# Two-layer hybrid encoder: late accumulating transfers behind a GpSimd copy, another order of two block products, halved memory attention, and small moves at the start and the end

## The chip, the cores and the metric

The kernel runs on one core of a Trainium2 chip. The metric is the device time of one execution in microseconds; the median of several runs counts. "PE" is the matrix engine, "PEld" its weight loads, DVE, ACT and POOL are the vector, scalar and GpSimd engines, and SP is the engine that only issues transfers. All shapes are partitions x elements, in float32 unless said otherwise.

## The reference

The reference computes two layers on 512 positions of width 2048. Each layer does, for h = rmsnorm(x):

```python
z = h @ w_in[l]                                   # 2048 -> 4928 columns
q_lat, kv_lat, k_pe, gb, gc, xin, q_mem, gate = split_cols(z)
a_out = mla_attention(q, k, v)                    # 8 heads over 512 keys, from the latents
c_out = short_gated_conv(gb, gc, xin, conv_w[l])  # gb * conv3(gc * xin)
m_out = memory_attention(q_mem, mem_n, w_mk, w_mv)  # 4 heads over 256 memory tokens
y = concatenate([a_out, c_out, m_out]) * silu(gate)
x = x + rmsnorm(y @ w_o[l])
```

The change leaves what is computed as it is.

## The kernel before, in words

**Numbers in two parts.** Each float32 operand of a matmul is split: ACT rounds it ("hi", `wh` for weights, line 212), DVE subtracts to get the rest ("lo", `wl`, line 216), and PE sums three products (`mm3s`, line 298).

**Units.** A unit is 256 rows of a weight block of 512 (or 416) columns, held as one 128x1024 tile `wr` of the pool `raw` (8 buffers). It costs PE 12 matmuls of 512 columns. `Program.run` goes through the steps in order; before a step it issues loads some units ahead (`load`, on the SP queue) and rounds units two steps ahead (`prep`). `wh` and `wl` have three buffers each, so rounding is also held to PE's pace.

**Seven products.** Every projection pair (five per layer) and both output projections multiply 2x2 blocks with seven products, P1 to P7, of four units each, instead of eight (`group`, line 473). The right-hand operands are sums of weight blocks. P5, P6 and P4 share the four tiles T: a second block is added to T in place before each use. For P7 the sum is a DVE addition of a freshly loaded tile (line 200); for P6 and P4 it is a transfer with accumulation that GpSimd issues (`more`, line 165). It is issued as soon as the earlier user of T is rounded (lines 217 to 218). The left-hand operands (S1 to S4, sums of activations) are made by deferred steps (`combine`), which `pr.until` forces out when a product needs them. P3 and P7 of one pair are interleaved unit by unit: P3 of rows 0, P7 of rows 0, P3 of rows 1, and so on; they share the tile B22, which P7 adds to after P3 has used it. The lists FIRST, HEAD and STEADY (lines 467 to 469) give the order of the products of a projection pair; SECOND and FOUR are those of the output projection.

**Order of engines.** PE, SP and POOL follow the written order. DVE and ACT are ordered by the scheduler of the framework, except at the start and in the output projection. Each engine's instructions run in order.

**Start.** `setup` builds an identity and issues five small constant transfers on ACT's queue. `first_load` (line 663) fetches x in half rows on SP; x tile 1 follows the squares of tile 0 in the program.

**Attention.** `head_iters` (line 1064) runs score, transposition and product with the values as a pipeline: scores of iteration k, transpositions of iteration k-3, and the product with V of the head that finished at k-5. The last rope head does that product in two halves of 256 queries (`halves`, line 1067).

**End.** `residual` (line 1301) normalises a 128-row tile of the output and adds it to x in two parts of 1024 columns. For the last tile the second part goes in two parts of 512, from a copy `o2` (lines 1268 to 1270).

Of the kernel before, what the change touches and what calls it, by code (L numbers as in the profile page):

```python
# [5 lines left out]
F32 = mybir.dt.float32  # L6
# [3 lines left out]
ALU = mybir.AluOpType  # L10
AX = mybir.AxisListType

P = 128
# [3 lines left out]
NT = S // P  # L17
MT = 256
HEADS = 8
# [44 lines left out]
class Unit:  # L64
# [2 lines left out]

    def __init__(self, key, loads=(), more=None, plus=None, alloc=None, gain=None, keep=None, other=None):  # L70
        self.key = key
        self.loads = loads
        self.more = more
        self.plus = plus
        self.alloc = alloc
        self.gain = gain
        self.keep = keep
        self.other = other
        self.behind = None


class Program:
# [40 lines left out]
    def run(self):  # L123
# [7 lines left out]
            users.setdefault(u.key, []).append(c)  # L131
        after = {a: b for cs in users.values() for a, b in zip(cs, cs[1:])}
        first_more = [c for c, u in enumerate(seq) if u.more is not None and users[u.key][0] == c]

        def move(engine, t, off, src, **kw):
            n = 1
# [51 lines left out]
        def prep(upto):  # L188
            while at["prep"] < min(upto, len(seq)):
                c = at["prep"]  # L190
                load(c + 1)
                while first_more and first_more[0] <= c + self.more_ahead:
                    load(first_more[0] + 1)
                    more(first_more.pop(0))
                u = seq[c]
                src = tiles[u.key]
                if any(e[0] == u.key for e in late):
                    flush()
                if u.plus is not None:
                    nc.vector.tensor_tensor(src, src, tiles[c], op=ALU.add)  # L200
                if u.other is not None:
                    nc.vector.tensor_tensor(src, src, tiles[u.other], op=ALU.add)
                at["prep"] += 1
                n = src.shape[-1]
                if u.alloc is None:
                    hi = hip.tile([P, 1024], F32R, tag="wh", name=f"wh{c}")
                    lo = lop.tile([P, 1024], F32R, tag="wl", name=f"wl{c}")
                else:
                    hi, lo = u.alloc()
                outs[c] = (hi[:, :n], lo[:, :n])  # L210
                if u.gain is None:
                    nc.scalar.copy(hi[:, :n], src)  # L212
                    flush()

                    def rest(c=c, n=n, src=src, hi=hi, lo=lo):
                        nc.vector.tensor_tensor(lo[:, :n], src, hi[:, :n].bitcast(F32), op=ALU.subtract)  # L216
                        if c in after and seq[after[c]].more is not None:
                            more(after[c])
                    late.append((u.key, rest))
                    if not self.lag:  # L220
                        flush()
                else:
                    flush()
                    for k, g in enumerate(u.gain()):
                        h = slice(k * (n // 2), (k + 1) * (n // 2))
                        nc.scalar.activation(hi[:, h], src[:, h], AF.Copy, scale=g)  # L226
                        nc.vector.scalar_tensor_tensor(lo[:, h], src[:, h], g, hi[:, h].bitcast(F32),  # L227
                                                       op0=ALU.mult, op1=ALU.subtract)
# [23 lines left out]
def encoder(tc, x, mem, positions, pre_norm_g, w_in, q_norm_g, w_uq, kv_norm_g, w_ukv, conv_w,  # L252
# [17 lines left out]
    banks = pool("banks", bufs=8, space=bass.MemoryType.PSUM)  # L270
    dram = pool("dram", space=bass.MemoryType.DRAM)
    pr = Program(nc, raw_p, hi_p, lo_p)
    add = pr.add

    G = {}
# [197 lines left out]
    def group(left, key, w, block, slot, passes, final, hold=None, by_two=False):  # L473
# [9 lines left out]
        def unit(q, c):  # L483
            def of(name, *loads, more=None, plus=None, alloc=None, **kw):
                return Unit((key, name, c), [block(h, j, c) for h, j in loads],
                            None if more is None else block(*more, c), None if plus is None else block(*plus, c), alloc,
                            **kw)
            if passes is FOUR and q in ("P5", "P6", "P7"):
                return {"P5": lambda: of("T", more=(0, 1)), "P6": lambda: of("T", other=(key, "B22", c)),
                        "P7": lambda: of("B22", plus=(0, 1))}[q]()  # L490
            if q == "P1":
                return of("P1" if apart else "T", (0, 0))
            if q == "P5":
                if passes is FIRST:
                    return of("T", (0, 0), more=(0, 1))
                return of("T", *([(0, 0)] if apart else []), plus=(0, 1))
            return {"P6": lambda: of("T", more=(1, 1)), "P4": lambda: of("T", more=(1, 0), alloc=hold),
                    "P2": lambda: of("P2", (1, 0)), "P3": lambda: of("B22", (1, 1)),
                    "P7": lambda: of("B22", plus=(0, 1))}[q]()

# [58 lines left out]
        def step(q, c):  # L559
            def f(*ops):  # L560
                if c == 0:
                    banks_for(q)
                if c < 3:
                    mm3s([p for tt in range(2) for p in products(q, c, tt, ops[0])])
                    return
                for tt in range(2):
                    mm3s(products(q, c, tt, ops[0]))
                    pr.flush()
                    ended(q, tt)
            return f  # L570
# [34 lines left out]
        for k, names in enumerate(passes):  # L605
            if names == ["P4"] and hold:
                for c in range(2):
                    out[2].insert(9 + 3 * c, (lambda ops, c=c: kept.__setitem__(c, ops), [unit("P4", c)], 0.0))
                out.append([(piece_of("P4", tt, c), [unit("P4", c)] if tt == 0 and c > 1 else [], 1.3 if c < 3 else 0.6)
                            for tt in range(2) for c in range(4)])  # L610
                continue
            steps = [(step(q, c), [unit(q, c)], room(q, c)) for c in range(4)
                     for q in (("P5", "P6", "P3", "P7") if passes is FOUR and k == 2 and c == 3 else names)]
            if "P7" in names and hold:
                steps[-3:] = [s + (n,) for s, n in zip(steps[-3:], (3, 3, 2))]
            if by_two and k == 0:
                steps[:2] = [(two(names[0], 0), [unit(names[0], c) for c in range(2)], 0.0, 1)]
            out.append(steps)
# [44 lines left out]
    def first_load(t):  # L663
        xt = G[f"x{t}"] = slab("x")
        if t < 2:
            for h in range(2):
                c = slice(h * 1024, (h + 1) * 1024)
                nc.sync.dma_start(xt[:, c], x[0, t * P:(t + 1) * P, c])
            return
        nc.sync.dma_start(xt, x[0, t * P:(t + 1) * P, :])  # L670

# [392 lines left out]
    def head_iters(j, rope, src, keys):  # L1064

        kts = keys // P
        halves = rope == HEADS - 1
        st = {}

        def score(t):  # L1070
# [25 lines left out]
        def trans(t):  # L1096
            def g():
                if halves and t % 2 == 0:
                    two = slab("PT", F32R).rearrange("p (s k c) -> p s k c", s=2, k=4)
                    st["PT"] = two[:, 0], two[:, 1]  # L1100
                    st["PT", t // 2] = st["PT"]
                if t == 0 and not halves:
                    if kts == 2:
# [127 lines left out]
    def out_proj(l):  # L1231
# [28 lines left out]
        def fin(g):  # L1260
            def f(i, j, tt):
# [3 lines left out]
                def scale():  # L1265
                    o = st["og"][t][:, cs]
                    nc.scalar.activation(G["junk"], o, AF.Square, scale=D ** -0.5, accum_out=st["ssq"][t][:, k:k + 1])
                    if last and t == NT - 1 and k == 2:
                        st["o2"] = scrap("o2")
                        nc.vector.tensor_tensor(st["o2"], o, st["g", g, j], op=ALU.mult)  # L1270
                    else:
                        nc.vector.tensor_tensor(o, o, st["g", g, j], op=ALU.mult)
                    st["n"][t] += 1
# [27 lines left out]
    def residual(l, st, t):  # L1301
# [9 lines left out]
        def part(c, n=1024):  # L1311
# [5 lines left out]
                    mybir.DependencyClass.Sync, mybir.DependencyReason.DATA), reason="the residual is there")  # L1317
                return
            xt = st["x"][t]
            o = st["o2"] if n == 512 and c == 1024 else og[:, cs]  # L1320
            nc.vector.scalar_tensor_tensor(xt[:, cs], o, st["r", t], xt[:, cs], op0=ALU.mult, op1=ALU.add)
            if last:
                nc.sync.dma_start(out[0][rows, cs], xt[:, cs])
# [4 lines left out]
            G[f"xo{t}"] = st["x"].pop(t), og  # L1328

        cost = 0.3 if last and t < 1 else 1.2  # L1330
        pr.defer(cost, lambda: part(0))
        if "o2" in st and t == NT - 1:
            pr.defer(0.7, lambda: part(1536, 512))
            pr.defer(0.7, lambda: part(1024, 512))
        else:
            pr.defer(cost, lambda: part(1024))
        if not last:
# [39 lines left out]
    def in_order(on):  # L1377
# [11 lines left out]
    first = ExitStack()  # L1389
    add(lambda: first.enter_context(tc.manual_schedule(  # L1390
        engines={mybir.EngineType.DVE, mybir.EngineType.Activation})))
    add(setup)
    for t in range(2):
        add(lambda t=t: first_load(t))
        add(lambda t=t: first_factor(t))
        if t == 0:
            add(lambda: first_rows(0))
# [178 lines left out]
```

## Time and profile before

| what | us |
|---|---|
| median of 3 runs (lowest, highest) | 1502.61 (1499.75, 1503.64) |
| the profiled execution, its own time | 1503.41 |
| its span, first to last instruction | 1501.6 |
| PE busy in it | 1478.9 |
| DVE busy | 1155.6 |
| ACT busy | 853.0 |
| POOL busy | 192.8 |

The mean granted clock of PE is 0.998 of full speed. Durations below come from the profiled execution, which was 0.8 us above the median. In rows of a timeline the first number is the start and the second how long the merged instructions lasted; square brackets hold the idle time of the engine just before and what ended it. Ends of matmuls are modelled.

### The profile page before, as it was taken

The page shows a single profiled execution, that of the slowest core. Times are in us where ns is not written, and L with a number is a line of the kernel's source. Part 1 is how long each engine was busy: PE and PEld are TensorE (multiplying, and loading weights), DVE is VectorE, ACT ScalarE, POOL GpSimd, SP SyncE. Part 2 cuts the span into 40 slices and gives each one's busy share as a digit, 9 for nine tenths or more (in the row PEclk, how much of TensorE's full clock was granted, in tenths as well). Part 3 has the DMA queues.
Part 4 walks back from the last instruction along what each step waited for, and adds up shares of the span by engine and source line. Part 5 has one row for each costly group of instructions (what it writes and reads, how often), then busy time and mean ns, then how long its engine had stood idle before and what let it go on. Part 6 is the DMA issues. An engine that isn't in the chain of part 4 may idle for free.

```text
span 1501.6 us, 19918 instructions
## 1 busy us (share of the span) xinstructions
PE 1478.9 (98%) x7345; PEld 1262.5 (84%) x7345; DVE 1155.6 (77%) x1504; ACT 853.0 (57%) x1313; POOL 192.8 (13%) x218
## 2 busy tenths in 40 slices
PE   8999999999999999999999999999999999999997
PEld 7878888997898888888888888888998888888885
DVE  6977877575878768887798877887586777788777
ACT  7643534454667668655498443534454677776453
POOL 1212020211000000011120112020221000002111
PEclk9999999999999999999999999999999999999999
DMA  8989695979577322399797899795969644027885
GB/s 312 231 217 220 192 192 163 195 199 237 167 239 197 98 45 69 96 215 272 221 347 226 229 223 219 196 195 154 202 198 201 196 113 113 29 85 152 272 195 138
DMA packets 156445, 280.03 MB, mean 186 GB/s; under 512 B 25928, under 2 KB 48556, under 8 KB 153388
## 3 DMA queue, kind: packets, MB, share of 16 engines
q1 hardware_dynamic: 118384, 194.82, 41.2%
q0 software_dynamic: 37808, 83.90, 28.7%
q8 instruction: 57, 0.93, 0.2%
q14 instruction: 40, 0.33, 0.1%
q10 hardware_dynamic: 156, 0.05, 0.0%
HBM read 259.33 MB, written 20.45 MB: 186 GB/s over the span
## 4 chain that ended last, share of the span: by engine, by line
PE 87%; DVE 4%; DMA 4%; issue 3%; ACT 2%; POOL 0%; DVEq 0%; POOLq 0%; ACTq 0%; SPq 0%
PE P L298 59%; PE o L298 4%; PE mk L298 3%; PE mv L298 3%; PE qps L298 3%; PE ptp L1111 2%; DMA wr<-in_w_in_dram 2%; PE tps L836 2%; PE vps L298 2%; PE kps L298 1%; PE qr L298 1%; DVE wl L216 1%; PE sc L1075 1%; PE sc L1076 1%; PE sc L1081 1%
## 5 line engine op out<-in xcount | busy, mean ns | idle before, releaser
L212 ACT CAST wh<-wr 128x1024 fp32r<-128x1024 f32 (+1 forms) x404 | 413.6, 1031 | 450.1 <-PE P L298 251.6
L216 DVE TENSOR_TENSOR wl<-wr,wh 128x1024 fp32r<-128x1024 f32 (+1 forms) x404 | 478.7, 1194 | 214.2 <-ACT wh L212 211.5
L298 PE MATMUL P<-wh,S 128*128 128x512 f32 (+1 forms) x1792 | 444.7, 385 | 1.6 <-DVE S L435 0.9
L298 PEld LDWEIGHTS P<-wh,S 128*128 128x128 f32 x1792 | 334.4, 188 | 61.4 <-DVE S L435 1.3
L298 PE MATMUL P<-wh,A 128*128 128x512 f32 (+1 forms) x1312 | 325.8, 385 | 0.8 <-ACT wh L212 0.6
L298 PEld LDWEIGHTS P<-wh,A 128*128 128x128 f32 x1312 | 244.8, 188 | 45.5 <-ACT wh L212 1.0
L298 PE MATMUL P<-wl,S 128*128 128x512 f32 (+1 forms) x896 | 243.7, 384 | 0.0
L298 PEld LDWEIGHTS P<-wl,S 128*128 128x128 f32 x896 | 168.0, 188 | 30.4
L298 PE MATMUL P<-wl,A 128*128 128x512 f32 (+1 forms) x656 | 178.6, 384 | 0.7 <-DVE wl L216 0.7
L142 POOL DMA_DIRECT2D wr<-in_w_in_dram x84 | 101.7, 1210 | 546.3 <-DVE wl L216 458.3
L298 PEld LDWEIGHTS P<-wl,A 128*128 128x128 f32 x656 | 123.0, 188 | 23.2 <-DVE wl L216 1.1
L200 DVE TENSOR_TENSOR wr<-wr,wr 128x1024 f32<-128x1024 f32 (+1 forms) x100 | 118.8, 1191 | 11.6 <-DMA wr<-in_w_in_dram 9.4
L1086 ACT ACTIVATE P<-sc,nm 128x512 f32<-128x512 f32 (+1 forms) x96 | 59.2, 618 | 46.2 <-DVE nm L1083 45.5
L1083 DVE TENSOR_REDUCE nm<-sc 128x1 f32<-128x512 f32 (+1 forms) x96 | 56.8, 593 | 8.5 <-PE sc L1081 8.4
L142 POOL DMA_DIRECT2D wr<-in_w_o_dram x32 | 38.7, 1208 | 191.1 <-DVE wl L216 144.2
L1092 ACT ACTIVATE P<-P,rec 128x512 f32<-128x512 f32 (+1 forms) x80 | 53.7, 681 | 7.2 <-DVE rec L1088 7.0
L226 ACT ACTIVATE wh<-wr,cols 128x512 fp32r<-128x512 f32 x64 | 42.5, 714 | 20.7 <-PE mv L298 8.6
L227 DVE SCALAR_TENSOR_TENSOR wl<-wr,cols,wh 128x512 fp32r<-128x512 f32 x64 | 45.0, 745 | 10.6 <-ACT wh L226 10.6
L1111 PE MATMUL ptp<-identr,P 128*128 128x128 f32 x320 | 50.0, 272 | 2.8 <-ACT P L1092 2.8
L1111 PEld LDWEIGHTS ptp<-identr,P 128*128 128x128 f32 x320 | 39.1, 140 | 10.9 <-ACT P L1092 3.3
L303 DVE TENSOR_TENSOR PTL<-ptp,PTH 128x512 fp32r<-128x512 f32 x56 | 37.8, 681 | 0.8 <-ACT PTH L302 0.8
L302 ACT CAST PTH<-ptp 128x512 fp32r<-128x512 f32 x56 | 32.4, 587 | 2.7 <-PE ptp L1111 2.0
(272 smaller groups left out, 1777.9 us busy)
## 6 DMA issues: line engine op xcount, KB each, us to landing
wr<-in_w_in_dram SPq DMA_DIRECT2D x172, 512.0 KB, 4.4
wr<-in_w_o_dram SPq DMA_DIRECT2D x72, 512.0 KB, 4.9
wr<-in_w_in_dram POOLq DMA_DIRECT2D x68, 512.0 KB, 7.2
wr<-in_w_in_dram SPq DMA_DIRECT2D x40, 416.0 KB, 3.3
wr<-in_w_o_dram POOLq DMA_DIRECT2D x32, 512.0 KB, 8.0
wr<-in_w_mk_dram SPq DMA_DIRECT2D x16, 512.0 KB, 7.0
wr<-in_w_mv_dram SPq DMA_DIRECT2D x16, 512.0 KB, 7.0
wr<-in_w_in_dram POOLq DMA_DIRECT2D x16, 416.0 KB, 5.6
```

The source lines that it names most:

```text
L142: engine.dma_start(dst, src, **kw)
L200: nc.vector.tensor_tensor(src, src, tiles[c], op=ALU.add)
L212: nc.scalar.copy(hi[:, :n], src)
L216: nc.vector.tensor_tensor(lo[:, :n], src, hi[:, :n].bitcast(F32), op=ALU.subtract)
L226: nc.scalar.activation(hi[:, h], src[:, h], AF.Copy, scale=g)
L227: nc.vector.scalar_tensor_tensor(lo[:, h], src[:, h], g, hi[:, h].bitcast(F32), op0=ALU.mult, op1=ALU.subtract)
L298: nc.tensor.matmul(ps, a[turn[0]], b[turn[1]], start=first and turn == (0, 0), stop=last and turn == ((1, 0) if late == 0 else (0, 1)), **kw)
L303: nc.vector.tensor_tensor(lo, src, hi.bitcast(F32), op=ALU.subtract)
L1083: nc.vector.tensor_reduce(nmax, ps, axis=AX.X, op=ALU.max, negate=True)
L1086: nc.scalar.activation(pt, ps, AF.Exp, bias=nmax, accum_out=tot)
L1092: nc.scalar.activation(pt, pt, AF.Copy, scale=rec)
L1111: nc.tensor.transpose(ps[:, k * P:(k + 1) * P], pt[:, k * P:(k + 1) * P], G["ident"])
```

## The change

Six things change.

1. Units of P4 in the projection pairs (FIRST, HEAD and STEADY) carry `put_off=6`. Their accumulating transfer is no longer issued when P6's unit is rounded, but when the unit six places before the P4 unit is about to be rounded. Ahead of it GpSimd copies one column (128x1) of the last rounded unit, so that its queue waits for that rounding.
2. Where the names are P3 and P7 alone, their units go in the order P3 0, P3 1, P7 0, P3 2, P7 1, P3 3, P7 2, P7 3.
3. In the first pair of the first layer, the operands S2 (S3 and S4) are forced out at the second unit of P5 (of P6) instead of the first unit of P6 (of P3 and P7).
4. Both x tiles are requested ahead of the constants, and the second half of tile 1 goes out on ACT's queue.
5. The memory heads do their product with V in halves too.
6. At the end the tile before the last is added in three parts as well, the third of them when the last tile's sum is being reduced.

```diff
@@ Program.run
+        hip_last = [None]
+        sums = [c for c, u in enumerate(seq) if u.put_off is not None and c not in first_more]
...
+                while sums and sums[0] <= c + seq[sums[0]].put_off:
+                    if any(e[0] == seq[sums[0]].key for e in late):
+                        flush()
+                    passed = self.small(1, "nm")
+                    nc.gpsimd.tensor_copy(passed, hip_last[0])
+                    more(sums.pop(0))
                 u = seq[c]
...
                 outs[c] = (hi[:, :n], lo[:, :n])
+                hip_last[0] = hi[:, :1].bitcast(F32)
...
-                        if c in after and seq[after[c]].more is not None:
+                        if c in after and seq[after[c]].more is not None and seq[after[c]].put_off is None:
                             more(after[c])
@@ group
-            return {"P6": lambda: of("T", more=(1, 1)), "P4": lambda: of("T", more=(1, 0), alloc=hold),
+            return {"P6": lambda: of("T", more=(1, 1)), "P4": lambda: of("T", more=(1, 0), alloc=hold,
+                                                                             put_off=6 if apart or passes is STEADY else None),
...
+                if passes is FIRST and q in ("P5", "P6") and c == 1:
+                    pr.until(lambda: all(left.there(LEFT[n], 0, tt) for n in (("P6",) if q == "P5" else ("P3", "P7"))
+                                         for tt in range(2)))
...
+            if names == ["P3", "P7"]:
+                order.sort(key=lambda e: (e[1] + (e[0] == "P7"), e[0]))
+            steps = [(step(q, c), [unit(q, c)], room(q, c)) for q, c in order]
@@ first_load
-            for h in range(2):
+            for h, by in ((0, nc.sync), (1, nc.sync if t == 0 else nc.scalar)):
                 c = slice(h * 1024, (h + 1) * 1024)
-                nc.sync.dma_start(xt[:, c], x[0, t * P:(t + 1) * P, c])
+                by.dma_start(xt[:, c], x[0, t * P:(t + 1) * P, c])
@@ head_iters
-        halves = rope == HEADS - 1
+        halves = rope is None or rope == HEADS - 1
...
-                    st["PT"] = two[:, 0], two[:, 1]
+                    st["PT"] = two[:, 0, :kts], two[:, 1, :kts]
@@ out_proj, residual
-                    if last and t == NT - 1 and k == 2:
+                    if last and t >= NT - 2 and k == 2:
...
+        if "rest" in st:
+            st.pop("rest")()
         pr.defer(cost, lambda: part(0))
-        if "o2" in st and t == NT - 1:
+        if ("o2", t) in st:
             pr.defer(0.7, lambda: part(1536, 512))
-            pr.defer(0.7, lambda: part(1024, 512))
+            if t == NT - 1:
+                pr.defer(0.7, lambda: part(1024, 512))
+            else:
+                st["rest"] = lambda: part(1024, 512)
@@ program
+    for t in range(2):
+        add(lambda t=t: first_load(t))
     add(setup)
     for t in range(2):
-        add(lambda t=t: first_load(t))
         add(lambda t=t: first_factor(t))
```

## Rows read from the trace of the kernel before

**Rows 1.** The page, part 1: busy time of each engine in the span.
```profile
PE 1478.9 (98%) x7345; PEld 1262.5 (84%) x7345; DVE 1155.6 (77%) x1504; ACT 853.0 (57%) x1313; POOL 192.8 (13%) x218
```

**Rows 2.** Waits of PE, whole span: who for whom, us, times, longest.
```profile
PE hps L643 <- DVE hs L689: 3.1, 1, 3.1
PE ptp L1111 <- ACT P L1092: 2.8, 2, 1.4
...
PE tps L836 <- ACT y L848: 1.2, 1, 1.2
PE P L298 <- DVE S L435: 0.9, 1, 0.9
PE P L298 <- DVE wl L216: 0.7, 1, 0.7
```

**Rows 3.** Timeline of the start, ACT.
```profile
12.81 1.06 ACT L678 ACTIVATE hs<-x 128x1024 f32<-128x1024 f32 x1 [3.17 <-DMA x<-in_x_dram]
...
14.29 1.04 ACT L212 CAST wh<-wr 128x1024 fp32r<-128x1024 f32 x1 [0.33 <-DMA wr<-in_w_in_dram]
```

**Rows 4.** Waits of SP's queue, 0 to 100 us, same columns.
```profile
SPq L668 <- DMA x<-in_x_dram: 3.7, 1, 3.7
```

**Rows 5.** Stretches: PE busy and count, clock, DMA share, GB/s.
```profile
6.00:8.00 2.00, 2.00 (x14) 1.00 0.80 252
...
24.00:26.00 2.00, 2.00 (x14) 1.00 1.04 384
```

**Rows 6.** Timeline at 79 us: PE waits for operand S2.
```profile
78.25 1.22 DVE L435 TENSOR_TENSOR S<-hT,S 128x1024 fp32r<-128x1024 f32 x1
...
79.52 0.30 PEld L298 LDWEIGHTS P<-wh,S 128*128 128x128 f32 x2 [1.29 <-DVE S L435]
```

**Rows 7.** Timeline at 372 us: ACT, then PE, in a P3/P7 pass.
```profile
371.60 1.04 ACT L212 CAST wh<-wr 128x1024 fp32r<-128x1024 f32 x1 [2.63 <-DVE wr L200]
...
373.20 0.66 PE L836 MATMUL tps<-identr,gm 128*128 128x128 f32 x4 [1.24 <-ACT y L848]
```

**Rows 8.** Timeline at 905 us: DVE, then PE, after a P3/P7 pass.
```profile
903.95 3.48 DVE L216 TENSOR_TENSOR wl<-wr,wh 128x1024 fp32r<-128x1024 f32 x3
...
905.22 1.20 PE L298 MATMUL P<-wl,A 128*128 128x512 f32 x4 [0.71 <-DVE wl L216]
```

**Rows 9.** Timeline at 476 us: PE among the memory heads.
```profile
475.64 0.44 PE L1111 MATMUL ptp<-identr,P 128*128 128x128 f32 x2 [1.43 <-ACT P L1092]
```

**Rows 10.** The chain that ended last: start, us, what (512 and 256 columns).
```profile
602.48 2.75 PE o L298 x12
622.26 3.01 PE o L298 x24
```

**Rows 11.** Timeline of the end: PE's last matmuls and DVE.
```profile
1489.91 2.48 DVE L1321 SCALAR_TENSOR_TENSOR xr<-og,r,xr 128x1024 f32<-128x1024 f32 x2 [0.68 <-POOL r L1309]
...
1490.60 0.61 PE L298 MATMUL P<-T4l,A 128*128 128x512 f32 x2
1492.31 0.68 DVE L501 TENSOR_TENSOR og<-og,P 128x512 f32<-128x512 f32 x1
...
1494.65 1.95 DVE L1321 SCALAR_TENSOR_TENSOR xr<-og,r,xr 128x1024 f32<-128x1024 f32 x2 [0.66 <-POOL r L1309]
```

**Rows 12.** Stretches of a STEADY group: PE, PEld, DVE, ACT, POOL, clock, DMA share, GB/s.
```profile
207.00:221.00 14.00, 14.00 (x67) 11.64 (x67) 12.50 (x15) 5.37 (x7) 4.84 (x4) 1.00 0.87 149
221.00:240.00 19.00, 19.00 (x86) 15.73 (x85) 13.36 (x12) 8.24 (x8) 0.00 (x0) 1.00 0.66 195
```

**Rows 13.** Forms of POOL: line, op, tiles, shapes, count; busy us, mean ns.
```profile
L307 POOL TENSOR_SCALAR ms<-st 128x1 f32<-128x1 f32 x8 | 3.3, 411 | 55.1 <-ACT mhs L624 27.7 <-ACT hs L624 15.6 <-ACT og L624 11.8
```

**Rows 14.** Transfers, KB, median us to landing: 60 to 80, then 150 to 170 us.
```profile
wr<-in_w_in_dram POOLq DMA_DIRECT2D x6, 512.0 KB, 7.7
wr<-in_w_in_dram SPq DMA_DIRECT2D x1, 512.0 KB, 11.0
...
wr<-in_w_in_dram SPq DMA_DIRECT2D x7, 512.0 KB, 3.6
```

More of the change, by code (lines that the diff above doesn't have):

```diff
@@ L64, with __init__ @@
 class Unit:
-    def __init__(self, key, loads=(), more=None, plus=None, alloc=None, gain=None, keep=None, other=None):
+    def __init__(self, key, loads=(), more=None, plus=None, alloc=None, gain=None, keep=None, other=None, put_off=None):
         self.key = key
@@ L79, in __init__ @@
         self.behind = None
+        self.put_off = put_off
 class Program:
@@ L272, in encoder @@
     pr = Program(nc, raw_p, hi_p, lo_p)
+    pr.small = lambda *a: small(*a)
     add = pr.add
@@ L611, in group @@
                 continue
-            steps = [(step(q, c), [unit(q, c)], room(q, c)) for c in range(4)
+            order = [(q, c) for c in range(4)
                      for q in (("P5", "P6", "P3", "P7") if passes is FOUR and k == 2 and c == 3 else names)]
+            if names == ["P3", "P7"]:
+                order.sort(key=lambda e: (e[1] + (e[0] == "P7"), e[0]))
+            steps = [(step(q, c), [unit(q, c)], room(q, c)) for q, c in order]
             if "P7" in names and hold:
@@ L1267, in scale @@
                     nc.scalar.activation(G["junk"], o, AF.Square, scale=D ** -0.5, accum_out=st["ssq"][t][:, k:k + 1])
-                    if last and t == NT - 1 and k == 2:
-                        st["o2"] = scrap("o2")
-                        nc.vector.tensor_tensor(st["o2"], o, st["g", g, j], op=ALU.mult)
+                    if last and t >= NT - 2 and k == 2:
+                        st["o2", t] = scrap("o2")
+                        nc.vector.tensor_tensor(st["o2", t], o, st["g", g, j], op=ALU.mult)
                     else:
@@ L1319, in part @@
             xt = st["x"][t]
-            o = st["o2"] if n == 512 and c == 1024 else og[:, cs]
+            o = st["o2", t] if n == 512 and c == 1024 else og[:, cs]
             nc.vector.scalar_tensor_tensor(xt[:, cs], o, st["r", t], xt[:, cs], op0=ALU.mult, op1=ALU.add)
```

## The prediction, as put on record before the result

> **What bounds the kernel now.** I read the page first: PE is busy for 1478.9 of 1501.6 us [rows 1], so no edit that leaves PE's work alone can bring more than the 22.7 us in which PE stands still, and a cheaper transfer or rounding is worth only what it takes out of those. The list of PE's waits comes second [rows 2]: the five rows at places that the change touches come to 3.1 + 2.8 + 1.2 + 0.9 + 0.7 = 8.7 us. The tail, where PE has finished, is the rest that matters: PE's last matmul ends at 1490.60 + 0.61 = 1491.2 and the span at 1501.6 [rows 1, 11], so some 10 us hang on DVE, POOL and the output transfers. Third, the timeline at each of these places, to see what PE waited for and what that in turn waited for. The sum below goes place by place. A measurement of this kernel can tell about 0.3%, 4.5 us, from no change.
>
> **The start.** PE waits 3.1 us for rows of x tile 1 [rows 2]. ACT, in order, idles 3.17 us until the last quarter of x lands at 12.8 us, squares it, and rounds the first weight at 14.29, having waited 0.33 us more for its transfer [rows 3]. That last quarter went out late: SP held it 3.7 us until another x transfer had landed [rows 4]; it was the ninth transfer of the two queues (four of x, five constants), so I read this as a limit of eight in flight. While it was held the transfer engines were poorly filled: 252 GB/s at 6 to 8 us against 384 later [rows 5]. Now it leaves with the first quarter, from ACT's queue. What this returns: a quarter is 0.52 MB, at 384 GB/s 1.4 us that the weights behind it are earlier. The squares are then no longer the bound, the first weight is. Ends: 3.1 us gained (all of PE's wait), 1.4 us lost (the ninth transfer is now another one, perhaps ahead of the first weight, and x tile 0 shares its bandwidth). I take -1.4, the quarter's own time, since ACT's 3.17 us of idling cover a later tile 0.
>
> What the Trainium skill says speaks against this part: "DMA: Bandwidth & Descriptors", section "Issuing engines are not separate DMA queues", has it that transfers started from several engines run on the same sixteen engines and interleave, so that a second queue saves only issue time. The row of SP's hold is why I don't follow it here: what is saved is a hold and not bandwidth. By that page of the Trainium skill the sum would lack this term.
>
> **S2 at 79 us.** PE waits 0.9 us for the low part of S2 [rows 2], written by a DVE instruction of 1.22 us that starts at 78.25 [rows 6]. Forcing the subtraction and the split out three units earlier (3 x 2.75 = 8 us, twelve 512-column matmuls taking 2.75 us [rows 10]) covers the wait: -0.9, ends -0.9 and 0. Late next would be P6's first sums, but none of PE's waits names them. S3 and S4 go the same way and cost nothing, because PE never waited for them; their DVE work is the same and only earlier.
>
> **The order of P3 and P7.** In the old order P7 adds to the tile that P3 has just used: cast, subtraction, addition, cast, subtraction hang together, and ACT's in-order queue stands behind it. At 372 us this shows in full: the cast waits 2.63 us for DVE's addition, a transposed gate's activation stands behind the cast, and PE waits 1.24 us for its bank [rows 7]. With a P3 unit between, addition and cast have one unit, 2.75 us, more than the 2.63: -1.2, ends -1.2 and 0. At 905 us DVE is behind with three subtractions after the sums that end P3 and P7, and PE waits 0.71 us [rows 8]. The new order ends P3 one unit earlier against P7, 2.75 us for the P3 half of that DVE work: -0.7, ends -0.7 and 0. The other ten passes of this kind (twelve in all) show no wait of PE, so there it is worth nothing.
>
> **Memory heads.** Halving costs PE: 24 matmuls of 256 columns took 3.01 us where 12 of 512 took 2.75 [rows 10], 0.13 us for the six of a head, 1.0 us for eight heads. It returns: six small ones (0.75 us) come two iterations earlier, in front of a transposition for which PE waited 1.43 us [rows 9], once a layer, 2.8 us in both [rows 2]. So 2 x 0.75 = 1.5 of the 2.8 are filled: net -0.5. Ends: -1.8 (the whole wait goes) and +1.0 (the halves come with ACT no faster). Each half takes a slab of its own, and never more than two are in use, as before.
>
> **The end.** DVE adds two 1024-column parts of the last tile but one, 2.48 us from 1489.91, and only then, at 1492.31, takes PE's last bank, 1.1 us after PE's end [rows 11]. Now 512 columns, some 0.6 us, move behind the last tile's reduction, into the 0.66 us in which DVE waits for POOL's factor [rows 11]. Gained 0.6, given back up to 0.2 and one more output transfer: -0.4, ends -0.6 and +0.5.
>
> **P4's late transfers.** Forty transfers move, five units later each, with forty copies. The copy is a 128x1 instruction; the nearest row has 0.41 us on POOL [rows 13]. It waits for ACT, and behind it in POOL's queue stands only its own transfer: the P6 transfers have landed by then, since their units are rounded. The rounding that reuses the copied buffer comes three units, 8 us, later. So the copies cost PE nothing as long as that 8 us stands; without it, 40 x 0.41 = 16 us at most. The landing: it is issued seven units ahead of its rounding, 19 us, and P6's and P4's took 7.7 [rows 14]: covered. No PE wait of before names a transfer, so nothing is gained either. I take 0; ends -1 and the slow rival below.
>
> **The sum**: -1.4 - 0.9 - 1.2 - 0.7 - 0.5 - 0.4 = **-5.1 us**. The profiled execution took 1503.4 us, so 1498.3; it stood 0.8 above the median of 1502.6, which gives **1497.5**. Its own range, with all gaining ends, goes down to -8.3 (1494.3), and up to about -2 (1500.6), since the losing ends would not all meet.
>
> **The rivals.**
> 1. *The start gains nothing*, because the transfer engines, not the queue, set when the first weight lands. For it: from 24 us on they run at 1.04 of their share [rows 5]. Against it: 0.80 while the quarter was held. The sum is then -3.7: 1498.9, no change that can be told. This is the time that the section of the Trainium skill named above would give.
> 2. *Slower: P7's loads land late.* Four accumulating transfers took 0.87 of 14 us [rows 12], 3.0 us of all engines each; their 149 GB/s x 14 us = 2.1 MB leave no room for any other load there. In the next 19 us 3.7 MB, seven loads, took 0.66, 1.8 us each. Now both meet in one P3/P7 pass of 22 us: 8 x 1.8 + 4 x 3.0 = 26.4 us of transfers. Place: a P7 load takes the buffer that the P7 sum before it frees, two units earlier in the new order. It is due after 5.5 us, and of the two units by which rounding leads PE, 5.5 us, the sum, the cast and the subtraction (1.2 + 1.0 + 1.2) leave 2. The point from which it decides is a landing of 7.5 us. Alone, loads took 3.6; beside accumulating transfers one took 11.0 [rows 14]. At 11.0, one late load in each of the four FIRST and HEAD passes costs 4 x 3.5 = 14 us: 1502.6 - 5.1 + 14 = 1511.5. Against it: accumulating transfers start one per unit, the later ones after half of the pass, and of the eight loads four land before it (T holds four of the eight buffers, the other four are filled ahead).
> 3. *The waits only move*: DVE is busy for 77% and its order is the scheduler's, so what leaves one place comes back at the next; 1502.6.
>
> **How the numbers follow.** Forecast 0.60, of which 0.44 lies below -4.5 us; the start for nothing 0.18, of which 0.04 is still below; P7's loads late 0.15; moved waits 0.07. So faster 0.44 + 0.04 = 0.48, slower 0.15, and the same 0.16 + 0.14 + 0.07 = 0.37. Likeliest is the forecast: 1497.5. The range takes in the forecast's bounds, the first rival and the third with the spread of the runs: 1494.0 to 1504.0; it leaves out the slow rival and some 0.05 below.
>
> **What would show it.** Right: the first weight rounded near 13 us; no wait for S at 79; no wait of PE for the gate's activation at 372 nor for `wl` at 905; some 0.7 us left in front of the transposition among the memory heads; DVE taking the last bank within 0.7 us of PE's end. P4's transfers stand among P7's loads, and those land within 7.5 us. Wrong: DVE additions of line 200 waiting for transfers, and PE behind them in the P3/P7 passes; ACT casts waiting for POOL's copy; the first weight still near 14.3 us.

## The result, and the profile after

The changed kernel took 1521.26 us (median; 1518.53 to 1523.37) where the kernel before took 1501.47 us beside it: a ratio of 1.0129, 95% interval 1.0115 to 1.0142. It is slower by some 19 us; 1497.5 us had been forecast. Each ratio below goes by runs of the kernel before made along with the kernel in question.

The page of the changed kernel, part 1, against [rows 1]:

```profile
PE 1488.7 (98%) x7393; PEld 1269.0 (83%) x7393; DVE 1153.6 (76%) x1505; ACT 850.2 (56%) x1313; POOL 229.1 (15%) x258
```

Its span is 1521.1 us, so PE stands still for 1521.1 - 1488.7 = 32.4 us (before: 22.7), and it is busy for 9.8 us more. The halves of the memory heads are 2.2 us of that at most (`o<-PT,Vm` in the groups by form: 15.3 us where 13.1 stood), and they don't make the difference: the kernel without copies below has them too, and PE is busy for 1478.7 us in it. The same work is done slower, of which more below.

The waits of PE in the changed kernel (who for whom, us, times, longest), against [rows 2]:

```profile
PE P L310 <- DVE wl L227: 13.2, 9, 3.4
PE hps L662 <- DVE hs L708: 3.2, 1, 3.2
...
PE ptp L1130 <- ACT P L1111: 1.4, 2, 0.7
PE tps L855 <- ACT y L867: 0.8, 1, 0.8
```

Two of the five old rows went as forecast: the wait for S is gone, and the one in front of the transposition is halved. The one for the gate's activation should have gone and is 0.8 us where it was 1.2. The start's wait has not moved. The new row, 13.2 us for the low halves of weights, leads to the loss. Behind it stand DVE's additions for P7, in part 5 of the page (busy, mean ns | idle just before):

```profile
L210 DVE TENSOR_TENSOR wr<-wr,wr 128x1024 f32<-128x1024 f32 (+1 forms) x100 | 119.0, 1190 | 91.4 <-DMA wr<-in_w_in_dram 81.5
```

DVE stood 81.5 us in front of them, waiting for a load. Before, the same wait came to 9.4 us in the list of DVE's waits (`DVE wr L200 <- DMA wr<-in_w_in_dram`, 8 times, longest 2.2).

The timeline of one such stretch, the P3/P7 pass of the second projection pair, on DVE, ACT and PE (SP's first row merges six loads):

```profile
146.60 19.15 SPq L146 DMA_DIRECT2D wr<-in_w_in_dram  x6
...
153.31 1.22 DVE L210 TENSOR_TENSOR wr<-wr,wr 128x1024 f32<-128x1024 f32 x1 [3.26 <-DMA wr<-in_w_in_dram]
...
158.66 1.05 ACT L223 CAST wh<-wr 128x1024 fp32r<-128x1024 f32 x1 [2.96 <-DMA wr<-in_w_in_dram]
...
161.38 1.23 DVE L210 TENSOR_TENSOR wr<-wr,wr 128x1024 f32<-128x1024 f32 x1 [4.43 <-DMA wr<-in_w_in_dram]
162.53 1.22 DVE L227 TENSOR_TENSOR wl<-wr,wh 128x1024 fp32r<-128x1024 f32 x1
...
163.80 1.22 PE L310 MATMUL P<-wl,S 128*128 128x512 f32 x2 [2.84 <-DVE wl L227]
```

Read it upwards from PE. It waits 2.84 us for the subtraction at 162.53, the low half of a unit of P3. That unit's cast is over at 158.66 + 1.05 = 159.71, so it isn't what the subtraction waits for. Ahead of the subtraction in DVE's order stands the addition of P7's next unit, and DVE idles 4.43 us in front of it until its load has landed. A late load of P7 so holds up the P3 unit ahead of it as well. That load went out at 154.56, just as the addition before it ended (153.31 + 1.22) and freed its buffer; and this addition had itself waited 3.26 us for the load of 146.60. The lateness is handed on from load to load. P4's transfers and P7's loads of these 15 us (queue and kind: packets, MB, share of the 16 engines' time; then the issues with their median us to landing, in the view of the transfers from 145 to 160 us):

```profile
q0 software_dynamic: 814, 1.57, 60.9%
q1 hardware_dynamic: 729, 1.43, 28.0%
...
wr<-in_w_in_dram POOLq DMA_DIRECT2D x4, 512.0 KB, 8.2
wr<-in_w_in_dram SPq DMA_DIRECT2D x4, 512.0 KB, 7.5
```

Before, six loads stood in these 15 us with no accumulating transfer issued among them, and the median to landing was 3.6 us; here four stand there, and it is 7.5. That median goes by the two of the four whose landing the trace has, 6.6 and 8.5 us; the other two went out at 154.56 and 156.98, and the additions that waited for them started at 161.38 and 164.13, some 7 us later.

### The profile page after: what moved, and what is told of

Read it like the earlier page. It is cut to its first block, busy times and chain, and to the rows that moved or that the text cites. A ratio compares the mean times of both kernels' runs of the same rounds, so it can differ in the third digit from the quotient of the medians.

```text
span 1521.1 us, 20089 instructions
## 1 busy us (share of the span) xinstructions
PE 1488.7 (98%) x7393; PEld 1269.0 (83%) x7393; DVE 1153.6 (76%) x1505; ACT 850.2 (56%) x1313; POOL 229.1 (15%) x258
## 4 chain that ended last, share of the span: by engine, by line
PE 83%; DMA 7%; DVE 5%; issue 2%; ACT 2%; POOL 0%; DVEq 0%; POOLq 0%; ACTq 0%
PE P L310 56%; DMA wr<-in_w_in_dram 7%; PE o L310 4%; PE mk L310 3%; PE mv L310 3%; PE qps L310 3%; PE ptp L1130 2%; DVE wl L227 2%; PE tps L855 2%; PE vps L310 2%; PE kps L310 1%; PE qr L310 1%; DVE wr L210 1%; PE sc L1094 1%; PE sc L1095 1%
## 5 line engine op out<-in xcount | busy, mean ns | idle before, releaser
L310 PE MATMUL P<-wl,S 128*128 128x512 f32 (+1 forms) x896 | 247.1, 388 | 11.6 <-DVE wl L227 11.4
L210 DVE TENSOR_TENSOR wr<-wr,wr 128x1024 f32<-128x1024 f32 (+1 forms) x100 | 119.0, 1190 | 91.4 <-DMA wr<-in_w_in_dram 81.5
L203 POOL COPY nm<-wh 128x1 f32<-128x1 f32 x40 | 37.3, 931 | 162.7 <-ACT wh L223 162.5
```

Source lines behind the costliest of these rows:

```text
L310: nc.tensor.matmul(ps, a[turn[0]], b[turn[1]], start=first and turn == (0, 0), stop=last and turn == ((1, 0) if late == 0 else (0, 1)), **kw)
```

## The experiments

Two questions came first: whether the postponed transfers cost the time alone or only together with the new order of P3 and P7, and what the start does. Four kernels answered them.

**P4's transfers early again.** The changed kernel with one argument undone, so that the copies go too:

```diff
-  put_off=6 if apart or passes is STEADY else None
+  put_off=None
```

> The changed kernel with P4's accumulating transfers issued at their old place and without the copies; all other parts stay. Theory A (the postponed transfers meet P7's loads, whose buffer now comes free only two units ahead; it takes both): nearly all of the 19.8 us lost go, 1498 to 1503 us, and DVE's additions wait under 15 us for transfers in the span instead of 81.5. Theory B (the new order of P3 and P7 alone starves P7's loads): stays at 1513 or more. Theory C (the copy, 0.93 us in the changed kernel against 0.41 expected, holds POOL or ACT): also falls to about 1500, but then the run without the copy's pacing differs; here A and C agree.

Measured: 1498.84 us, ratio 0.9991 (0.9981 to 1.0). The whole loss is gone. What missed is the figure for DVE: its additions still wait 32.5 us for loads, and PE does not feel it.

**The postponement alone**, on the kernel before: change 1 and nothing else.

> The kernel before with the postponed P4 transfers and their copies alone; old order of P3 and P7. Theory A: the loads of the old order have their buffer three to four units ahead, so they bear landings of 8 to 11 us better: 1502 to 1508 us, well below the changed kernel's 1521. Theory B: no loss, 1501.5. Theory C or a variant of A in which the postponement alone is enough: 1515 to 1522.

Measured: 1519.64 us, ratio 1.0133 (1.0103 to 1.0163). The postponement with its copies costs all of it, in the old order of P3 and P7 as well. The waits of ACT in this kernel (who for whom, us, times, longest):

```profile
ACT wh L223 <- DVE wr L210: 109.9, 38, 5.8
ACT wh L223 <- DMA wr<-in_w_in_dram: 48.3, 20, 4.7
...
ACT wh L223 <- POOL nm L203: 12.9, 5, 2.8
```

The first row is no sign of lateness: in the kernel before it came to 119.6 us. What grew are ACT's waits for loads (31.0 us before), DVE's additions waiting for them (31.3 us, 9.4 before), and PE's waits for `wh` and `wl`, 7.6 and 7.5 us. Here the cast also waits five times for POOL's copy, a sign the prediction had named, and three times in the next kernel (7.4 us); in the changed kernel it never does.

**The changed kernel in the old order of P3 and P7:**

```diff
-            if names == ["P3", "P7"]:
-                order.sort(key=lambda e: (e[1] + (e[0] == "P7"), e[0]))
```

> The changed kernel with the old order of P3 and P7; transfers still postponed behind the copies. Theory A: 1499 to 1507 us. Theory B: 1496 to 1499. Postponement alone or the copies: stays at 1515 to 1521. The wait of PE for the gate's activation (1.24 us before, 0.8 in the changed kernel) should be back at about 1.2 if the new order is what shortened it.

Measured: 1520.65 us, ratio 1.0136 (1.0121 to 1.0152), no different from the changed kernel. The new order neither makes the loss nor lessens it.

**The start alone**, on the kernel before: change 4 and nothing else.

> The kernel before with the changed start alone (both x tiles ahead of the constants, the last quarter on ACT's queue). If the start as such costs: the constant that is now the ninth transfer holds ACT's queue until 7 to 8 us, the table load stands behind it, PE reaches the first pair's second half 0.7 us later, 1502.2 us, same within what can be told. If the start's loss in the changed kernel came from elsewhere: ACT's first square stays near 5.8 us and the first rounding comes at 13 us or before, 1500 us.

Measured: 1503.26 us, ratio 1.0022 (1.0013 to 1.0031): the new start loses 3.3 us (2.0 to 4.7).

What about the postponement does the harm was open: the copies and their queue, or the transfers that now meet P7's loads. The next four kernels tell these apart.

**No copies.** The transfers keep their place in the program, but nothing holds GpSimd's queue any more:

```diff
-                    passed = self.small(1, "nm")
-                    nc.gpsimd.tensor_copy(passed, hip_last[0])
                     more(sums.pop(0))
```

> The changed kernel without the column copies: P4's transfers still stand at the later place in GpSimd's program, but nothing holds them, so GpSimd issues each as soon as its own queue is free and the P6 user of the tile is rounded, mostly right behind P6's. Theory A (the cost is that P4's transfers fall among P7's loads and slow them): 1499 us, as with the transfers issued early, since the copies are what places them; DVE's additions wait about 33 us for transfers and PE waits under 1 us for wl in a P3/P7 pass. Rival B (the written place alone is enough, for example because the queue of P4's transfers is passed by those of P6): about 1520.

Measured: 1498.62 us, ratio 0.9988 (0.9977 to 1.0). The transfers go out early and the loss is gone: the copies are what sets the time of issue. This kernel differs from the changed one by nothing else, so it is the one to set beside it. PE's busy time is 1478.7 us here for the same 7393 matmuls, its span 1497.6: of the 23.5 us between the two spans, 10.0 are matmuls that took longer and 13.5 are PE standing still.

**The same places and copies, an eighth of the bytes** (the rest of the second block is left out of the sum):

```diff
+            if u.put_off is not None:
+                dst = tiles[u.key].rearrange("p (a b) -> p a b", b=u.more.shape[2])
+                nc.gpsimd.dma_start(dst[:, :, :64], u.more[:, :, :64], accum_op=ALU.add)
+                return
             move(nc.gpsimd, tiles[u.key], 0, u.more, accum_op=ALU.add)
```

> The changed kernel, copies and places as they are, but each postponed transfer brings only the first 64 of its 512 (or 416) columns; the rest of that operand's sum is left out. Theory A (bandwidth: half a megabyte of accumulating transfer beside P7's loads): 1499 us, DVE's additions wait under 40 us for transfers, no PE wait for wl above 1.5 us in P3/P7 passes. Rival B (the copies, their waits for ACT and the order of GpSimd's queue cost the time, whatever the bytes): 1518 to 1521. In between, say 1505 to 1512, if the number of descriptors rather than the bytes counts (64 columns are 256 bytes a piece).

Measured: 1499.17 us, ratio 0.9994 (0.9983 to 1.0005); DVE's additions wait 22.4 us. Copies, their waits for ACT, places and the number of transfers are all as in the changed kernel, and there is no loss. So it is the bytes, in the new order; no run tries the copies alone in the old order, where ACT waits 12.9 us for them.

**Three units earlier:** `put_off=9` in the place of 6.

> The changed kernel with put_off 9 in the place of 6: each postponed transfer goes three units (8 us) earlier, so that it meets P3's half of the pass more than P7's. Theory A: the additions of P7 wait less for their loads: between 1499 and 1515, about 1508. Rival B (copies cost, at whatever place): 1520, as at 6.

Measured: 1505.51 us, ratio 1.0035 (1.0023 to 1.0047); DVE's additions wait 59.2 us. Against the same kernel with early transfers (0.9991) that is 0.0044, 6.6 us, where a put_off of 6 costs 0.0138, 20.7 us: 8 us of place take away two thirds of the loss.

**The same bytes, places and copies, without accumulation** (the transfer overwrites the tile, so P6's block is left out):

```diff
+            if u.put_off is not None:
+                dst = tiles[u.key].rearrange("p (a b) -> p a b", b=u.more.shape[2])
+                nc.gpsimd.dma_start(dst, u.more)
+                return
```

> The changed kernel, copies, places and bytes as they are, but each postponed transfer overwrites the tile in the place of adding to it (P6's block is then missing from that operand). If any half megabyte in that place does the harm: 1518 to 1521, as with adding. If it is the price of accumulation (3.0 us of all transfer engines for 512 KB against 1.8 for a plain load): 1500 to 1508, and DVE's additions wait 35 to 50 us for transfers in the place of 81.

Measured: 1503.88 us, ratio 1.0026 (1.0015 to 1.0038); DVE's additions wait 54.0 us, a little over what was expected. Of the 0.0138 only 0.0035 are left: some three quarters of the loss go with the adding. The view of the transfers from 145 to 160 us of this kernel shows it, beside the rows of the changed kernel above:

```profile
q1 hardware_dynamic: 1241, 2.41, 48.4%
q0 software_dynamic: 576, 2.10, 42.0%
...
wr<-in_w_in_dram SPq DMA_DIRECT2D x6, 512.0 KB, 4.6
wr<-in_w_in_dram POOLq DMA_DIRECT2D x3, 512.0 KB, 5.6
```

Plain, GpSimd's queue moved 2.10 MB in 42.0% of 15 us, 3.0 us of all engines for a megabyte. Adding, it moved 1.57 MB in 60.9%, 5.8 us for a megabyte. SP's loads took 2.9 to 3.0 in both. The adding transfer takes twice the engines' time per byte, and P7's loads get what is left. One more thing differs here: the plain transfers went out in larger packets, 2.10 MB in 576 where 1.57 MB took 814. SP's plain loads, 1.43 MB in 729, are as small as the adding ones and cost what the large ones cost, which speaks for the adding; plain packets of that size on GpSimd's own queue were not run.

The same pass in stretches of 22 us tells what PE made of it (PE, PEld, DVE, ACT, POOL busy; clock; DMA share; GB/s), first the changed kernel, then the one without accumulation, then the one without copies:

```profile
146.00:168.00 22.00, 19.16 (x78) 15.25 (x77) 13.80 (x14) 7.59 (x7) 6.18 (x7) 0.92 0.95 233
```
```profile
146.00:168.00 22.00, 22.00 (x98) 18.21 (x97) 17.26 (x19) 9.67 (x11) 4.04 (x6) 1.00 0.87 293
```
```profile
146.00:168.00 22.00, 22.00 (x99) 18.21 (x97) 16.85 (x18) 10.50 (x12) 0.00 (x0) 1.00 0.76 227
```

The changed kernel has the fullest engines (0.95) and moves less (233 GB/s) than the one that does not add (293 at 0.87).

**The start undone too**: transfers early and the x tiles requested as before.

```diff
-            for h, by in ((0, nc.sync), (1, nc.sync if t == 0 else nc.scalar)):
+            for h, by in ((0, nc.sync), (1, nc.sync)):
...
-    for t in range(2):
-        add(lambda t=t: first_load(t))
     add(setup)
     for t in range(2):
+        add(lambda t=t: first_load(t))
```

> Two parts undone: P4's transfers issued early again and the old start; the new order of P3 and P7, S2, the halved memory heads and the end stay. If the start costs 1.7 us as measured alone: 1497.1 (the kernel with early transfers and the new start had 1498.8, the kernel before 1500.8), ratio about 0.9975. If the start's loss is absorbed later: 1498.8, ratio 0.999.

Measured: 1495.6 us, ratio 0.9975 (0.9966 to 0.9985), the lower of the two forecasts; the start's loss stays lost. This version beats both kernels.

**The new start with its ninth transfer on GpSimd** (transfers early):

```diff
-        nc.scalar.dma_start(rows[m + 4 * depth:], kv_norm_g.rearrange("l (k p) -> (l k) p", p=P))
+        nc.gpsimd.dma_start(rows[m + 4 * depth:], kv_norm_g.rearrange("l (k p) -> (l k) p", p=P))
```

> The changed kernel with P4's transfers early and the new start, but the ninth transfer (kv_norm's rows) issued by GpSimd in the place of ACT. Theory (the new start loses because the ninth transfer of SP and ACT stands in ACT's in-order queue ahead of its first square, and ACT is what starts the work): ACT's first square near 6 us and not 8.9, and the whole 1494 to 1497, that is 2 to 4 us below the same kernel with that transfer on ACT (0.9991 of the kernel before) and at or below the one with the old start (0.9975). Rival (the second half of x tile 1 lands late for bandwidth, whoever issues the constants): no better than 0.9991.

Measured: 1497.53 us, ratio 0.9984 (0.9975 to 0.9993): between the two, and its interval meets both neighbours', so the time alone doesn't tell the two theories apart. The trace shows a part of each. ACT at the start (start, us, instruction, [idle before <- releaser]), first the changed kernel, then this one, then the one with the old start:

```profile
7.65 1.28 ACT L697 ACT_TABLE_LOAD   x1 [7.65 <-DMA x<-in_x_dram]
```
```profile
3.53 1.28 ACT L697 ACT_TABLE_LOAD   x1 [3.53 <-issue]
7.48 1.06 ACT L697 ACTIVATE hs<-x 128x1024 f32<-128x1024 f32 x1 [2.66 <-DMA x<-in_x_dram]
```
```profile
4.75 1.06 ACT L697 ACTIVATE hs<-x 128x1024 f32<-128x1024 f32 x1 [0.45 <-DMA x<-in_x_dram]
...
10.24 1.06 ACT L697 ACTIVATE hs<-x 128x1024 f32<-128x1024 f32 x1 [1.68 <-DMA x<-in_x_dram]
```

In the changed kernel ACT, which issues the ninth transfer, is held until the first x has landed, and even its table comes only at 7.65. Moving that transfer brings the first square from 8.94 to 7.48, but the old start has it at 4.75: the first quarter of x itself lands later. That four quarters share the engines from the start where three did is the likely reason; no run tries it by itself. The last quarter gains nothing by leaving early: in this kernel's trace it is there at 10.30, in the old start's at 10.22.

**The old order too**: transfers early, old start, old order. What is left of the change is S2, the halved heads and the end.

> P4's transfers early, the old start and the old order of P3 and P7; S2, halved memory heads and the end stay. If the new order is worth the 1.9 us that the prediction gave it: ratio 0.9975 + 0.0013 = 0.9988, and PE's wait of 1.2 us for the gate's activation at 372 us is back; if it is worth nothing: 0.9975.

Measured: 1495.96 us, ratio 0.9975 (0.9966 to 0.9985), the same as with the new order. No worth of the order shows; the two intervals leave room for some 2 us either way. PE's wait for the gate's activation is indeed back at 1.2 us (0.8 with the new order); against that DVE's additions wait only 8.6 us for loads, not 28.4.

## Why the prediction was wrong, step by step

**P4's late transfers: costed at 0, measured 20.7 us** (0.0138, the ratios of the changed kernel and of the one with early transfers). This is the step that failed. The prediction looked at whether the moved transfer lands in time for its own user, and it does: in the pass above the four land 10 to 16 us before their P4 units are rounded (the last at 165.2 us for a rounding at 175.6). What it does to the loads beside it was put into the slow rival, with a chance of 0.15. The rival had the place right (P7's loads beside accumulating transfers, in the P3/P7 passes of FIRST and HEAD). The landing of 7.5 us from which it decides is near: in the pass above PE waits at landings of 6.6 to 8.5, and the trace has single loads of 8.4 and 9.5 us in the passes of the second layer. What it lacked is that the lateness is handed on from load to load, and that a late addition holds the subtraction of the P3 unit ahead of it. It had the size nearly: 14 us. Comparing the times at which the same units are rounded in the changed kernel and in the one without copies, the gap grows by 7.8 us over the first two passes, by 12.4 over the first two of the second layer, and by 4.4 over the rest of the kernel.

Its working was wrong in two places. It put the lateness down to the new order, which frees a buffer only two units ahead; with the old order the loss is the same (1.0136). And its argument against itself, that the later adding transfers come after half of the pass and four of the eight loads land before them, doesn't hold: in the pass above three of the four are issued at 145.61, 148.50 and 150.07 us, and the loads of the last three P7 units at 146.60, 154.56 and 156.98, right behind or among them. The sum of the rival, 26.4 us of transfers in a pass of 22, spoke for a larger chance than 0.15; its 4 x 3.0 us of adding transfers is the term that the runs confirm.

**What the prediction had no term for: PE slows down after it has stood still.** Stretches of 4 us in the same kind of pass of the second layer, in the changed kernel (same columns as above):

```profile
952.00:956.00 4.00, 3.62 (x16) 2.65 (x15) 0.12 (x1) 0.86 (x1) 1.30 (x2) 1.00 1.08 286
956.00:960.00 4.00, 1.19 (x4) 0.67 (x4) 1.58 (x2) 0.43 (x2) 0.00 (x0) 0.88 1.06 254
960.00:964.00 4.00, 3.17 (x8) 2.50 (x9) 3.16 (x4) 1.88 (x3) 0.00 (x0) 0.50 0.50 141
964.00:968.00 4.00, 4.00 (x15) 3.24 (x14) 3.70 (x5) 3.41 (x5) 0.00 (x0) 0.76 0.95 312
```

PE has work for 1.19 of 4 us, waiting for a subtraction behind an addition that waits for its load; then the granted clock is 0.50, the lower level of 1.2 GHz, and eight matmuls fill 3.17 us where sixteen filled 3.62 in the first of these stretches. In stretches of 1 us the clock is 0.50 from 959 to 966 here, from 164 to 167 behind the wait of 2.84 us in the pass shown first, and from 901 to 904 after one of 2.83 us that ends at 899.5. PE is busy for some 11 us at this level; half of that, 5 to 6 us by this estimate, is what the clock made of the 10.0 us of longer matmuls. The rest lies in small pieces elsewhere, mostly at a clock of 1.00, and no run shows its cause.

**The start: -1.4 forecast, +3.3 measured** (2.0 to 4.7), outside its ends. The prediction followed the last quarter of x, in front of which ACT idled longest [rows 3], and took SP's hold [rows 4] for a loss. The chain runs through tile 0: its two squares, its factor on POOL, then DVE's scaling, from which PE transposes. DVE's scaling in the kernel with the old start (and order), the one with the ninth transfer on GpSimd, and the one with early transfers and the new start:

```profile
8.44 1.42 DVE L706 TENSOR_SCALAR hs<-x,r 128x1024 f32<-128x1024 f32 x2 [6.88 <-POOL r L699]
```
```profile
11.36 1.42 DVE L708 TENSOR_SCALAR hs<-x,r 128x1024 f32<-128x1024 f32 x2 [9.80 <-POOL r L701]
```
```profile
12.30 1.42 DVE L708 TENSOR_SCALAR hs<-x,r 128x1024 f32<-128x1024 f32 x2 [10.74 <-POOL r L701]
```

By this reading the hold that the change removes had kept tile 1 out of tile 0's way. PE, idle for longer, is slowed as well: from 14 to 20 us its granted clock is 0.65 and 0.83 in the two kernels with the new start, 1.00 in the one with the old. The ninth transfer, which the prediction had as a bound of 1.4 us on the losing side, holds not its own queue but ACT, whose squares stand behind it. The Trainium skill, "DMA: Bandwidth & Descriptors", section "Issuing engines are not separate DMA queues", says that transfers of all engines interleave on the same sixteen; the prediction set that aside, and the landings here (first square at 7.48 for 4.75, last quarter no earlier) agree with it. A caution on the method: in the profiled execution of the kernel before, the first x landed at 5.8 us and the last quarter at 12.8, in three others with the old start at 4.7 to 4.8 and at 9.3 to 10.2. So the rows from which the term was sized, the 252 GB/s of [rows 5] among them (387 in the last kernel above), were in part one execution's.

**S2: -0.9 forecast, -1.2 seen.** PE's list of waits has no row for S any more, and in the last kernel above, against the kernel before, the units behind that place are rounded 1.2 us earlier than those ahead of it.

**The order of P3 and P7: -1.9 forecast, 0 measured** (0.9975 with and without, to some 2 us). At 372 us 0.4 of the 1.2 us of waiting went: the cast no longer waits for DVE's addition but for PE, and the gate's activation still stands behind it. The 0.7 us for `wl` at 905 us was never the order's: the last kernel above, with the old order, has no such row either, nor has the kernel before with the new start alone. P7's additions wait longer for loads in the new order (28.4 us for 8.6), but no wait of PE shows behind them.

**Memory heads: -0.5 forecast, about -1.7 seen**, near the gaining end of -1.8. PE's wait fell from 2.8 to 1.4 us, and in the last kernel above the units behind the memory heads gain 0.8 us in each layer on those of the kernel before. The matmuls of 256 columns are there as counted, 96 of them where 48 of 512 stood.

**The end: -0.4 forecast, -0.7 seen.** PE's end and DVE's taking of the last bank:

```profile
1510.77 0.61 PE L310 MATMUL P<-T4l,A 128*128 128x512 f32 x2
...
1511.42 0.69 DVE L514 TENSOR_TENSOR og<-og,P 128x512 f32<-128x512 f32 x1
```

DVE is there as PE ends, not 1.1 us later [rows 11]; from PE's end to the span's it is 1521.1 - 1511.4 = 9.7 us and was 10.4.

**The copies: 0 and confirmed, at another size.** On POOL, by form (count; busy us, mean ns; idle before):

```profile
L203 POOL COPY nm<-wh 128x1 f32<-128x1 f32 x40 | 37.3, 931 | 162.7 <-ACT wh L223 162.5
```

One took 0.93 us on the mean, not the 0.41 of [rows 13]. That PE does not feel them in the new order is shown by the kernel with an eighth of the bytes.

So the parts that stay without the postponement and the new start come to 0.25% (0.15 to 0.34), 3.7 us, where their terms of the sum were 0.9 + 0.5 + 0.4 = 1.8. The prediction's lower bound of -8.3 leaves out the -1 that it gave the transfers; nothing hangs on it.

## What to carry to other kernels

Cost a moved transfer by what it takes from the transfers that it comes to stand among, in engine time per byte at its own rate, and not only by whether it lands in time for its own user; a pass whose transfers add up to more than its length deserves the larger chance. Ask also what stands behind the late instruction on its engine: here a late load of one product held up the other. A queue that waits may be doing useful pacing: before removing a hold, see who gets the bandwidth in the meantime and whether he is earlier in the chain. And the start of a single profiled execution should be compared with another execution's before a term is sized from it.

## What the runs showed of the hardware that was not expected

A transfer that adds to its target took twice the transfer engines' time per byte of a plain one on the same queue, between the same memories and in the same place (5.8 and 3.0 us for a megabyte; the plain ones in larger packets, and SP's plain loads in small ones at 2.9 to 3.0). The prediction had both durations (3.0 and 1.8 us for half a megabyte), from passes apart, but no row of before showed what the one does to the other. And waits of PE of 2.8 to 3.4 us in the P3/P7 passes cost more than their length: about them the granted clock was 0.50 for some 3 us twice and some 7 us once. Not every such wait does it: the kernel before waited 3.1 us at the start, and its clock was 1.00 from 14 to 22 us.
